# One large buffer more, one split weight tile less, and a changed order, in a hybrid trunk on one core

## The chip, the core and the metric

The kernel runs on one NeuronCore of a Trainium2 chip. The metric is the device time of one execution in microseconds; the median of three runs is given. TensorE (PE) multiplies, VectorE (DVE) and ScalarE (ACT) do the elementwise work, GpSimd (POOL) some small work, SyncE (SP) issues nearly all DMAs.

## What is computed

One layer of a decoder trunk for 512 positions of width 1024, in fp32. A mixer has three branches of width 512 (RG-LRU, gated DeltaNet, S5), each projected, gated and summed. After it come cross-attention into 256 memory positions and a gated MLP with a causal convolution, each with a residual. Cut to the mixer and the memory:

```python
xa, ga, q, k, v, z, beta, alpha, uc, gates = split(h @ w_in)
ya = rg_lru(conv(xa) + b) * gelu(ga)                 # branch 0
o = delta_rule(l2norm(q), l2norm(k), v, g, beta)     # branch 1: per chunk a unit lower triangular solve
yb = rmsnorm(o, b_norm) * silu(z)
yc = gelu(s5(uc)); yc = yc * sigmoid(yc @ w_glu)     # branch 2
x = x + sum(sigmoid(gates) * (branches @ w_branch)) @ w_out
k, v = split(rmsnorm(mem, mem_norm) @ w_kv)          # cross-attention
```

## The kernel before, in words

All weights are 179 tiles of 128x1024 fp32 (512 KB each), in the order of `weight_order()`. SP streams them into a pool `raw` of 3 buffers. ACT rounds a tile into `whi`, DVE takes the rest, raw minus `whi`, into `wlo`; each pool has `WB` buffers. A product is three passes on PE (high by high, high by low, low by high), so a full tile is 24 matmuls of 128x512. `wnext` gives the next tile to PE and splits ahead by `WB - 1` tiles; a split waits until PE is done with the tile that held its buffer.

Large intermediates (8 KB in each partition) live in `NS` slots of one pool, handed out in the order of the program; whoever takes a slot waits for the last reader of what was in it. Small ones of 128x512 come from a pool of 10.

The program text is one run of products (`group`); the S5, RG-LRU, delta and memory parts are Python generators that `pump` advances between the products, by the microseconds that they `yield`. So constants such as `XW`, `HRW` and `MY` say how far along the products the next piece of a side part is put, and Tile's scheduler then sets the order on each engine. Each engine works its own list in that order.

Around the change the order of products is: S5 inputs, keys, queries, values, the RG-LRU inputs XA and GA (tiles 17 to 24), then for each branch `gate` tiles (results `gu`) and `br` tiles (results `psb`). Branch 0 comes first, then branch 2, then the memory's keys (`wk`, `ps_wk`) and values (`wv`, `psv`), the Z tiles and branch 1. Meanwhile on the side:
- `rglru` makes ya: two small products pr and pi, then a chain over ACT (`rg`) and DVE that ends in `yah` and `yal`.
- `s5` writes its kernel `kd` to DRAM and reads it back as a Toeplitz matrix T, forms the states H on DVE, and then multiplies T by U and F by H into `py`.
- `delta` transposes keys, queries and values (`trp`), forms pk and pq per head, solves the triangles on DVE (block substitution in `nBX`, written to DRAM as dX), and later does the rest of the solve on PE (Qp, Zp), the scan over chunks (m, vn, Sp, op), a norm (`oss`), and transposes back (`tro`).
- `mem_prep` waits for the substitution (`sub_done`), loads the memory in one transfer on ACT's DMA queue into a slot, splits it to `mgh` and `mgl`, and makes the norm (`macc`, `rtm`, `rbp`).

```python
mt = self.slot("mem")
nc.scalar.dma_start(out=mt, in_=self.ap["memT"])
```

Of the kernel before, what the change touches and what calls it, by code (L numbers as in the profile page):

```python
# [10 lines left out]
ALU = mybir.AluOpType  # L11
# [3 lines left out]

GA_N = (1, 2, 0)

CH = 1.14
LV = 0.91
XW = 20.0  # L20
VW = 13.0
GW = 20.0
SPD = 30.0
NW = 24.0
MY = 8.0
RW = 9.69
IY = 2.0
VY = 2.41
RY = 2.6
M0 = 2.86  # L30
HY = 2.79
HRW = 7.0
TY = 2.0

NS, NP, WB = 17, 2, 4
WARM = 6
# [3 lines left out]
def weight_order():  # L40
    o = [("uc", t) for t in range(4)]
    for b in (K_, Q_, V_):
        o += [("in", b + t) for t in range(4)]
        if b == Q_:
            o.insert(-3, ("ba",))
    for t in range(4):
        o += [("in", XA + t), ("in", GA + t)]
    for br in (0, 2, 1):
        gt = lambda mp: [("gate", br * 8 + 2 * mp), ("gate", br * 8 + 2 * mp + 1)]
        ahead = GA_N[br]  # L50
        first = [k for mp in range(ahead) for k in gt(mp)]
        if br == 1:
            o += [("wk", m) for m in range(8)]
            o += [("wv", c, kp) for c in range(2) for kp in range(4)]
            o += [("in", Z_ + t) for t in range(4)]
        o += first
        if br == 2:
            o += [("glu", 0), ("glu", 1)]
        for mp in range(4):
            o += (gt(mp) if mp >= ahead else []) + [("br", br, mp)]  # L60
    o += [("out", m) for m in range(8)]
    o += [("wq", m) for m in range(8)]
    o += [("wo", m) for m in range(8)]
# [34 lines left out]
class Kern:  # L98
# [124 lines left out]
    def wnext(self, key, ahead=WB - 1):  # L223
        i = self.wi
        assert ORDER[i] == key, (ORDER[i], key)
        self.wi += 1
        self.w_split(i + 1 + ahead)
        self.w_dma(self.split_i + 2)
        return self.wt.pop(i)
# [156 lines left out]
    def mixer(self, x, xg, rb, pss, par5):  # L386
# [64 lines left out]
        for i in range(4):  # L451
# [6 lines left out]
            self.act(ga, ps, AF.Gelu_apprx_tanh)  # L458
            rgs.append(self.start(self.rglru(i, xf, ga)))
        hbg = cp.tile([128, 24], F32, name="hbg")  # L460
        self.gs(hbg, self.par("b_gate"), 0.5)
        macc = [self.slot("macc0"), self.slot("macc1")]
        mv = lambda m: macc[m // 4][:, (m % 4) * 512:(m % 4 + 1) * 512]
        def gates(br, mp):
            tg = []
            for j in range(2):
                m = 2 * mp + j
                ps = self.group([("gate", br * 8 + m)], h)[0]
                u = self.t512("gu")
                self.act(u, ps, AF.Tanh, scale=0.5, bias=hbg[:, br * 8 + m:br * 8 + m + 1])  # L470
                tg.append(u)
            return tg

        for br in (0, 2, 1):
# [12 lines left out]
            else:  # L487
# [3 lines left out]
                self.mem_values()  # L491
                self.z = self.slot("z")
                for i in range(4):
                    ps = self.group([("in", Z_ + i)], h)[0]
                    self.act(self.z[:, i * 512:(i + 1) * 512], ps, AF.Silu)
                self.z_done = True
                tgs = [gates(br, mp) for mp in range(GA_N[1])]
# [44 lines left out]
    def delta(self):  # L542
# [5 lines left out]

        ktok, vtok = self.slot("ktok"), self.vraw
        ss = sm("ss", 32)  # L550
        for ti, (src, dst) in enumerate(((self.kraw, ktok), (self.qraw, None), (self.vraw, vtok))):
            for h in range(4):
# [4 lines left out]
                if ti < 2:  # L557
                    jk = self.t512("junk")
                    for n in range(4):
                        c = slice(n * 128, (n + 1) * 128)  # L560
                        self.act(jk[:, c], ps[:, c], AF.Square,
                                 accum_out=ss[:, ti * 16 + h * 4 + n:ti * 16 + h * 4 + n + 1])
                if ti != 1:
                    self.act(hv(dst, h), ps)
# [12 lines left out]
        while not self.s5_done:  # L577
            yield

        keT, qeT, kdec = self.kraw, self.qraw, ktok  # L580
        nA, qk = self.slot("nA"), self.slot("qk")
# [3 lines left out]
        yield RW  # L585
        for h in range(4):
            R = E = hv(Rs, h)
            D, DT = self.t512("D"), self.t512("DT")
# [14 lines left out]
            for n in range(4):  # L603
                c = slice(n * 128, (n + 1) * 128)
                self.stt(un(nA, h, n), pk[:, c], nbr[:, h * 4 + n:h * 4 + n + 1], D[:, c], ALU.mult, ALU.mult)
            self.tt(hv(qk, h), pq, DT, ALU.mult)
            self.act(gt[:, h * 4:h * 4 + 4], E[:, 127::128])
            self.tt(hv(qeT, h), hv(qeT, h), E, ALU.mult)
# [36 lines left out]
        for b in range(4):  # L645
            for s in range(2):
                c = 32 * b + 16 * s
                nc.gpsimd.dma_start(out=xv[32 * b:32 * b + 32, :, c:c + 16], in_=dX[s, :, b].rearrange("u i j -> i u j"))
        Z = self.slot("Zi")
        self.gz(Z[:, :1])  # L650
        self.sub_done = True
# [112 lines left out]
        self.tt(o3, o3, rqn, ALU.mult)  # L764
        while not self.z_done:
            yield
        yb = self.kslots("yb", 4)
# [108 lines left out]
    def rglru(self, i, xf, ga):  # L876
        nc = self.nc
        c = slice(i, i + 1)
        wg = self.wg[i % 2]
        yield 4  # L880
        pr, pi = self.psd("pr"), self.psd("pi")
# [179 lines left out]
    def s5(self):  # L1061
# [9 lines left out]
        Q1, Q2 = self.s5Q  # L1071
        self.act(CC[up], CC[up], scale=-1.0)
        yield VW
        Vt = self.slot("Vt0")
        G = self.s5G
        for e in range(4):
# [8 lines left out]
            yield 2.6  # L1085
            if e == 0:
                U = self.slot("U")
                udv = ud.rearrange("(q s) c j n -> s c j q n", s=2)
                for s in range(2):
                    for j in range(4):  # L1090
                        self.sd.dma_start(out=U[64 * s + 16 * j:64 * s + 16 * j + 16, :].rearrange("c (q n) -> c q n", n=128),
                                            in_=udv[s, :, j])
        c4 = self.s5P[:, :64].rearrange("p (o i q) -> p o i q", o=2, i=2)
# [46 lines left out]
        for q in range(16):  # L1140
            self.mm(pk[:, q * 32:(q + 1) * 32], Vt[:, q * 128:(q + 1) * 128], CC[:, q * 32:(q + 1) * 32], True, True)
            if q % 2:
                yield 1.3
        ks = self.t512("ks")
        self.act(ks, pk)
# [8 lines left out]
        for k, e in ((0, 0), (1, 0), (0, 1), (1, 1)):  # L1154
# [6 lines left out]
            for s, rows in enumerate((lo, up)):  # L1161
                self.tt(f5[k][rows, s, q8], ta[rows], tb[rows], ALU.add)
            yield 2.6

        for n, top in ((16, 32), (32, 63)):
# [4 lines left out]
        for e in range(4):  # L1170
            q4 = slice(4 * e, 4 * e + 4)
            ta, tb, tg = (self.t512(n).rearrange("p (o q n) -> p o q n", o=2, q=4) for n in ("ra", "rb5", "rg5"))
            b2 = lambda t: t[:, q4].unsqueeze(1).to_broadcast([128, 2, 4, 64])
# [9 lines left out]
            for o in range(2):  # L1183
                nc.vector.tensor_tensor_scan(out=fl(tg[:, o]), data0=fl(D), data1=fl(wd[:, o, q4]),
                                             initial=0.0, op0=ALU.mult, op1=ALU.add)
            yield TY
            self.tt(ta, b2(C), tg, ALU.mult)
            self.tt(tb, b2(S), tg[:, ::-1], ALU.mult)
            self.tt(wd[:, 0, q4], ta[:, 0], tb[:, 0], ALU.subtract)
            self.tt(wd[:, 1, q4], ta[:, 1], tb[:, 1], ALU.add)  # L1190
            yield TY
        T = self.slot("T")
        self.gz(T, 0.0)
        t5 = T.rearrange("p (q s t d) -> p s q t d", q=16, s=2, t=4)
        for s in range(2):
            for j in range(4):
                r0 = 64 * s + 16 * j
                self.sd.dma_start(out=t5[r0:r0 + 16, s, :, j:], in_=kv[s, :, :, 0:4 - j])
        yield HRW
# [3 lines left out]
        for e in range(4):  # L1203
# [16 lines left out]
            for u in range(4):  # L1220
                c = slice((4 * e + u) * 128, (4 * e + u + 1) * 128)
                d = slice(u * 128, (u + 1) * 128)
                self.mm(ps[:, d], T[:, c], U[:, c], True, False)
                self.mm(ps[:, d], F[0][:, c], H[0][:, d], False, False)
                self.mm(ps[:, d], F[1][:, c], H[1][:, d], False, True)
                yield 0.65
# [242 lines left out]
    def mem_prep(self):  # L1469
        nc = self.nc  # L1470
        while not self.sub_done:
            yield
        yield M0
        mg = self.kslots("mg", 8, 256)
        acc = self.t512("macc")[:, :256]
        mt = self.slot("mem")
        nc.scalar.dma_start(out=mt, in_=self.ap["memT"])
        yield MY
        for k in range(0, 8, 2):
            yield 1.0  # L1480
            for j in range(2):
                xk = mt[:, (k + j) * 256:(k + j + 1) * 256]
                ins = self.split(*mg[k + j], xk, self.par("g_mem")[:, k + j:k + j + 1])
                if k + j == 0:
                    self.tc.keep_in_program_order(ins)
                self.sumsq(acc, k + j, xk, 8, 256)
        self.mg = mg
# [148 lines left out]
```

## Time and profile before

| what | value |
|---|---|
| median of three runs | 1098.15 us (1096.86 to 1098.66) |
| profiled execution, its own time | 1102.97 us |
| its span | 1101.2 us |
| PE busy | 1064.3 us, 97% |
| DVE, ACT, POOL busy | 704.1, 503.3, 149.4 us |
| DMA | 112.30 MB, mean 102 GB/s |

The profiled execution has its own time, beside the span that the engines' records cover. A busy PE can run at either of two clocks; the views give the granted clock of a stretch as a share of full speed (1.00 is 2.4 GHz, and 0.50 would be 1.2 GHz throughout).

### The profile page before, as it was taken

The page shows a single profiled execution, that of the slowest core. Times are in us where ns is not written, and L with a number is a line of the kernel's source. Part 1 is how long each engine was busy: PE and PEld are TensorE (multiplying, and loading weights), DVE is VectorE, ACT ScalarE, POOL GpSimd, SP SyncE. Part 2 cuts the span into 40 slices and gives each one's busy share as a digit, 9 for nine tenths or more (in the row PEclk, how much of TensorE's full clock was granted, in tenths as well). Part 3 has the DMA queues.
Part 4 walks back from the last instruction along what each step waited for, and adds up shares of the span by engine and source line. Part 5 has one row for each costly group of instructions (what it writes and reads, how often), then busy time and mean ns, then how long its engine had stood idle before and what let it go on. Part 6 is the DMA issues. An engine that isn't in the chain of part 4 may idle for free.

```text
span 1101.2 us, 13592 instructions
## 1 busy us (share of the span) xinstructions
PE 1064.3 (97%) x5150; PEld 888.8 (81%) x5150; DVE 704.1 (64%) x1044; ACT 503.3 (46%) x810; POOL 149.4 (14%) x286
## 2 busy tenths in 40 slices
PE   9999998899998799999999999999999999999996
PEld 7778876688886798888888887888888888888886
DVE  6887589937998545356464546487774247777434
ACT  7555676736522435443344435364442124444224
POOL 7898801100001000000000000000000000000003
PEclk9999999899999789999999999999999999999998
DMA  7552222145324313322352112223232322223212
GB/s 251 180 136 78 78 72 77 50 108 199 106 96 142 108 58 115 116 77 96 103 168 93 60 37 96 97 95 97 99 99 100 103 97 97 96 95 96 96 39 77
DMA packets 45633, 112.30 MB, mean 102 GB/s; under 512 B 10608, under 2 KB 18432, under 8 KB 45184
## 3 DMA queue, kind: packets, MB, share of 16 engines
q1 hardware_dynamic: 45168, 110.13, 31.3%
q10 hardware_dynamic: 144, 1.05, 0.3%
q8 instruction: 40, 0.66, 0.2%
q0 software_dynamic: 256, 0.26, 0.1%
q14 instruction: 25, 0.20, 0.1%
HBM read 106.56 MB, written 4.86 MB: 101 GB/s over the span
## 4 chain that ended last, share of the span: by engine, by line
PE 82%; DVE 6%; POOL 5%; DMA 3%; issue 2%; ACT 1%; SPq 0%; DVEq 0%; ACTq 0%; POOLq 0%
PE ps_up L156 24%; PE psdn L156 12%; PE ps_gate L156 9%; PE ps_in L156 7%; PE psb L156 4%; PE ps_wq L156 4%; PE ps_out L156 4%; PE ps_wo L156 4%; POOL s5p L785 3%; PE ps_wk L156 3%; PE psv L156 2%; PE pv L156 2%; DVE wlo L144 1%; PE sc L156 1%; POOL s5p L150 1%
## 5 line engine op out<-in xcount | busy, mean ns | idle before, releaser
L141 ACT ACTIVATE whi<-raw 128x1024 fp32r<-128x1024 f32 (+1 forms) x185 | 189.8, 1030 | 296.5 <-PE psdn L156 79.3
L144 DVE TENSOR_TENSOR wlo<-raw,whi 128x1024 fp32r<-128x1024 f32 (+1 forms) x185 | 219.6, 1192 | 160.4 <-ACT whi L141 153.0
L156 PE MATMUL ps_up<-xgh,wlo 128*128 128x512 f32 x384 | 149.8, 390 | 0.0
L156 PE MATMUL ps_up<-xgh,whi 128*128 128x512 f32 x384 | 149.5, 389 | 0.0
L156 PE MATMUL ps_up<-xgl,whi 128*128 128x512 f32 x384 | 149.4, 389 | 0.0
L144 POOL TENSOR_TENSOR acc<-acc,sq 128x256 f32<-128x256 f32 x11 | 8.3, 752 | 719.8 <-ACT sq L141 719.2
L156 PEld LDWEIGHTS ps_up<-xgh,wlo 128*128 128x128 f32 x384 | 72.1, 188 | 15.2 <-issue 0.2
L156 PEld LDWEIGHTS ps_up<-xgh,whi 128*128 128x128 f32 x384 | 72.1, 188 | 15.0 <-issue 0.2
L156 PEld LDWEIGHTS ps_up<-xgl,whi 128*128 128x128 f32 x384 | 72.1, 188 | 15.0
L156 PE MATMUL psdn<-actl,whi 128*128 128x512 f32 (+1 forms) x216 | 78.9, 365 | 0.0
L156 PE MATMUL psdn<-acth,wlo 128*128 128x512 f32 (+1 forms) x216 | 78.9, 365 | 0.0
L156 PE MATMUL psdn<-acth,whi 128*128 128x512 f32 (+1 forms) x216 | 78.8, 366 | 0.0
L156 PE MATMUL ps_gate<-hh,whi 128*128 128x512 f32 x192 | 76.0, 396 | 1.9 <-ACT gu L141 1.9
L156 PE MATMUL ps_gate<-hh,wlo 128*128 128x512 f32 x192 | 75.6, 394 | 0.0
L156 PE MATMUL ps_gate<-hl,whi 128*128 128x512 f32 x192 | 75.4, 393 | 0.0
L153 DVE SCALAR_TENSOR_TENSOR fu<-pad,par,fu 128x512 f32<-128x512 f32 x96 | 71.5, 748 | 1.8 <-ACT fu L141 0.3
L156 PE MATMUL ps_in<-hh,whi 128*128 128x512 f32 x168 | 68.1, 406 | 0.0
L156 PE MATMUL ps_in<-hh,wlo 128*128 128x512 f32 x168 | 67.2, 400 | 0.0
L156 PE MATMUL ps_in<-hl,whi 128*128 128x512 f32 x168 | 66.9, 398 | 0.0
L144 DVE TENSOR_TENSOR pad<-ps_up,rb 128x512 f32<-128x512 f32 x48 | 32.8, 688 | 43.9 <-PE ps_up L156 42.7
L156 PEld LDWEIGHTS psdn<-actl,whi 128*128 128x128 f32 x216 | 40.7, 189 | 6.6
L156 PEld LDWEIGHTS psdn<-acth,whi 128*128 128x128 f32 x216 | 40.7, 189 | 6.5
(383 smaller groups left out, 2225.9 us busy)
## 6 DMA issues: line engine op xcount, KB each, us to landing
raw<-wts SPq DMA_DIRECT2D x177, 512.0 KB, 3.5
x<-xT SPq DMA_DIRECT2D x16, 256.0 KB, 4.2
out<-x SPq DMA_DIRECT2D x7, 256.0 KB, 2.4
raw<-wts SPq DMA_DIRECT2D x8, 128.0 KB, 4.6
BC<-bc SPq DMA_DIRECT2D x1, 1024.0 KB, 8.1
ud<-uperm SPq DMA_DIRECT2D x4, 256.0 KB, 5.3
U<-ud SPq DMA_DIRECT2D x8, 128.0 KB, 6.0
yd<-T SPq DMA_DIRECT2D x8, 128.0 KB, 3.1
```

The lines of the kernel that those rows point to most:

```text
L141: return self.nc.scalar.activation(out=out, in_=in_, func=func, **k)
L144: return (eng or self.nc.vector).tensor_tensor(out=out, in0=a, in1=b, op=op)
L150: return e.tensor_scalar(out=out, in0=a, scalar1=s1, scalar2=s2, op0=op0, op1=op1)
L153: return self.nc.vector.scalar_tensor_tensor(out=out, in0=a, scalar=s, in1=b, op0=op0, op1=op1)
L156: return self.nc.tensor.matmul(out, lhsT=lhsT, rhs=rhs, start=start, stop=stop)
L785: return self.pin(self.nc.gpsimd.tensor_tensor(out=out, in0=a, in1=b, op=op))
```

## The change

- Buffers: `NS` goes from 17 to 18 slots, `WB` from 4 to 3, and the DMA of weights runs one tile less ahead of the split.
- The four Z tiles are multiplied after the second pair of XA and GA tiles.
- Two pairs of gate tiles, not one, stand ahead of the first `br` tile of branch 0; four of these gate results are kept in a slot `tga`.
- The keys' slot `ktok` is taken later; the keys are transposed a second time (`trk`, 4 transposes a head) in the loop that makes pk and pq. The four ACT copies move along.
- T is taken and cleared right behind the S5 kernel's product, and its eight loads are issued from ACT's queue, not SP's. The products of `py` start with F and H. U is loaded earlier.
- The memory is loaded in four transfers into four small tiles; its split goes into two slots (`mg0`, `mg1`) that hold high and low parts side by side.
- Yield constants change (XW 20 to 30, VW 13 to 10, NW 24 to 20, IY 2.0 to 1.6, HRW 7 to 4, TY 2.0 to 2.4, two yields in place of waits), and one S5 temporary goes.

```diff
-GA_N = (1, 2, 0)
+GA_N = (2, 2, 0)
-NS, NP, WB = 17, 2, 4
+NS, NP, WB = 18, 2, 3
...
         o += [("in", XA + t), ("in", GA + t)]
+        if t == 1:
+            o += [("in", Z_ + t) for t in range(4)]
...
             o += [("wv", c, kp) for c in range(2) for kp in range(4)]
-            o += [("in", Z_ + t) for t in range(4)]
         o += first
...
         self.w_split(i + 1 + ahead)
-        self.w_dma(self.split_i + 2)
+        self.w_dma(self.split_i + 1)
         return self.wt.pop(i)
...
             rgs.append(self.start(self.rglru(i, xf, ga)))
+            if i == 1:
+                self.z = self.slot("z")
+                for j in range(4):
+                    ps = self.group([("in", Z_ + j)], h)[0]
+                    self.act(self.z[:, j * 512:(j + 1) * 512], ps, AF.Silu)
+                self.z_done = True
         hbg = cp.tile([128, 24], F32, name="hbg")
...
+        tga = self.slot("tga")
...
-                u = self.t512("gu")
+                u = tga[:, m * 512:(m + 1) * 512] if br == 0 and m < 4 else self.t512("gu")
...
-                if ti != 1:
+                if ti == 2:
                     self.act(hv(dst, h), ps)
...
+        ktok = self.slot("ktok")
...
+            pt = self.psd("trk")
+            for n in range(4):
+                self.tr(pt[:, n * 128:(n + 1) * 128], un(self.kraw, h, n))
...
             self.tt(hv(qk, h), pq, DT, ALU.mult)
+            self.act(hv(ktok, h), pt)
...
+        T = self.slot("T")
+        self.gz(T, 0.0)
...
+        t5 = T.rearrange("p (q s t d) -> p s q t d", q=16, s=2, t=4)
+        for s in range(2):
+            for j in range(4):
+                r0 = 64 * s + 16 * j
+                nc.scalar.dma_start(out=t5[r0:r0 + 16, s, :, j:], in_=kv[s, :, :, 0:4 - j])
...
-                self.sd.dma_start(out=t5[r0:r0 + 16, s, :, j:], in_=kv[s, :, :, 0:4 - j])
...
-                self.mm(ps[:, d], T[:, c], U[:, c], True, False)
-                self.mm(ps[:, d], F[0][:, c], H[0][:, d], False, False)
-                self.mm(ps[:, d], F[1][:, c], H[1][:, d], False, True)
+                self.mm(ps[:, d], F[0][:, c], H[0][:, d], True, False)
+                self.mm(ps[:, d], F[1][:, c], H[1][:, d], False, False)
+                self.mm(ps[:, d], T[:, c], U[:, c], False, True)
...
-        yield M0
-        mg = self.kslots("mg", 8, 256)
+        sl = [self.slot(f"mg{i}", F32R) for i in range(2)]
+        mg = [tuple(sl[k // 4][:, (2 * (k % 4) + z) * 256:(2 * (k % 4) + z + 1) * 256] for z in range(2)) for k in range(8)]
         acc = self.t512("macc")[:, :256]
-        mt = self.slot("mem")
-        nc.scalar.dma_start(out=mt, in_=self.ap["memT"])
+        ms = [self.t512("mem") for _ in range(4)]
+        for i, m in enumerate(ms):
+            nc.scalar.dma_start(out=m, in_=self.ap["memT"][:, i * 512:(i + 1) * 512])
         yield MY
-        for k in range(0, 8, 2):
-            yield 1.0
-            for j in range(2):
-                xk = mt[:, (k + j) * 256:(k + j + 1) * 256]
-                ins = self.split(*mg[k + j], xk, self.par("g_mem")[:, k + j:k + j + 1])
-                if k + j == 0:
-                    self.tc.keep_in_program_order(ins)
-                self.sumsq(acc, k + j, xk, 8, 256)
+        for k in range(8):
+            xk = ms[k // 2][:, k % 2 * 256:(k % 2 + 1) * 256]
+            ins = self.split(*mg[k], xk, self.par("g_mem")[:, k:k + 1])
+            if k == 0:
+                self.tc.keep_in_program_order(ins)
+            self.sumsq(acc, k, xk, 8, 256)
+            if k % 2:
+                yield 1.0
+        self.gz(self.Zi[:, :1])
         self.mg = mg
         rt, _ = self.rstd([acc], n=256, bc=False)
         yield RY

```

How that moves instructions shows in the lists of the engines. On PE, at the first branch product of the program before (`whi_1741` is a gate tile, `whi_1802` the first `br` tile, weight 27):

```order
L156 MATMUL ps_gate<-hl_436,whi_1741 128x512
L156 MATMUL ps_gate<-hh_434,wlo_1742 128x512
L156 MATMUL psb<-yah_1274,whi_1802 128x512
L156 MATMUL psb<-yal_1275,whi_1802 128x512
L156 MATMUL psb<-yah_1274,wlo_1803 128x512
L156 MATMUL pr<-xfga,wg_695 128x512
```

After the change the gate tiles (`whi_2022` is the third, weight 31) lead to `py`, and the first `br` tile (`whi_2166`, weight 33) stands behind the last `py`:

```order
L157 MATMUL ps_gate<-hh_426,whi_2022 128x512
L157 MATMUL ps_gate<-hl_428,whi_2022 128x512
L157 MATMUL py_2040<-H_1997,F_1350 128x128
L157 MATMUL py_2040<-H_1998,F_1351 128x128
L157 MATMUL py_2040<-U,T 128x128
...
L157 MATMUL py_2256<-U,T 128x128
L157 MATMUL psb<-yah_1257,whi_2166 128x512
L157 MATMUL psb<-yal_1258,whi_2166 128x512
```

Before, `psb` came after two gate tiles and `py` later, between other tiles; after, the four Z tiles and three gate tiles come first, then `py` among the fourth, then `psb`.

On ACT, at the memory's load before (`whi52` and `whi53` are weights of the memory's keys, `gu` gate results; what a row waits for stands in brackets, DMAHW1 in the first DMA row is the landing of dX):

```order
L141 ACTIVATE whi52_3113<-raw52_3035 128x1024 [waits DMAHW5_49,DVE_49,PE_49]
L141 ACTIVATE gu_3110<-ps_gate_3073,hbg_1862 128x512 [waits PE_49]
L141 ACTIVATE whi53_3158<-raw53_3078 128x1024 [waits DMAHW6_49,DVE_49,PE_49]
L141 ACTIVATE gu_3156<-ps_gate_3112,hbg_1862 128x512 [waits PE_49]
L1477 DMA mem_3174<-memT 128x2048 [waits DMAHW1_49,DVE_49]
L141 ACTIVATE whi54_3248<-raw54_3117 128x1024 [waits DMAHW7_49,PE_49,Activation_49]
L141 ACTIVATE mgh0_3171<-mem_3174,par_84 128x256 [waits DMAHW2_49]
```

and after (`whi51` is a `br` tile, `whi54` the last one of branch 2; DMAHW5 in the `mg1` row is the landing of dX):

```order
L142 ACTIVATE gu_3067<-ps_gate_3030,hbg_2016 128x512 [waits PE_49]
L1484 DMA mem_3115<-memT 128x512
L1484 DMA mem_3116<-memT 128x512
L1484 DMA mem_3117<-memT 128x512
L1484 DMA mem_3118<-memT 128x512 [waits DVE_49]
L142 ACTIVATE whi51_3133<-raw51_3073 128x1024 [waits DMAHW4_49,DVE_49,PE_49]
L142 ACTIVATE mg0_3112<-mem_3115,par_84 128x256 [waits DMAHW7_49]
...
L142 ACTIVATE gu_3241<-ps_gate_3165,hbg_2016 128x512 [waits DVE_49,PE_49]
L142 ACTIVATE mg1_3113<-mem_3117,par_84 128x256 [waits DMAHW5_49,DVE_49]
L142 ACTIVATE mg1_3113<-mem_3117,par_84 128x256
L142 ACTIVATE mg1_3113<-mem_3118,par_84 128x256 x2
L142 ACTIVATE whi54_3292<-raw54_3247 128x1024 [waits DMAHW3_49,PE_49]
```

The transfers and half of the split moved four gate and branch tiles ahead; `mg1`, which takes the slot of `nBX`, still stands behind dX, and `whi54` behind `mg1`.

On PE, at the memory's norm before (`whi_3248` is weight 54, a tile of the memory's keys):

```order
L156 MATMUL ps_wk<-mgh_3171,whi_3248 128x256
L156 MATMUL ssp<-cst,macc 128x1 x2
L156 MATMUL ps_wk<-mgl_3172,whi_3248 128x256
L156 MATMUL ps_wk<-mgh_3171,wlo_3249 128x256
L156 MATMUL rbp<-diag,cst 128x256
L156 MATMUL Qp<-Zi,nA 96x64 x16
```

and after (`whi_3166` and `whi_3243` are gate tiles 52 and 53, `whi_3292` is the `br` tile 54, `whi_3325` the first tile of the memory's keys):

```order
L157 MATMUL ps_gate<-hh_426,whi_3166 128x512
L157 MATMUL ssp<-cst,macc 128x1 x2
L157 MATMUL ps_gate<-hl_428,whi_3166 128x512
...
L157 MATMUL ps_gate<-hh_426,whi_3243 128x512
L157 MATMUL rbp<-diag,cst 128x256
L157 MATMUL ps_gate<-hl_428,whi_3243 128x512
...
L157 MATMUL psb<-ych_2740,wlo_3293 128x512
L157 MATMUL ps_wk<-mg_3112,whi_3325 128x256 x2
```

The two small products of the norm, `ssp` and `rbp`, moved from the middle of the keys' tiles to the gate tiles ahead of them.

## Rows read from the trace of the kernel before

**Rows 1.** The page, busy time (share of the span) and instructions of the engines.
```profile
PE 1064.3 (97%) x5150; PEld 888.8 (81%) x5150; DVE 704.1 (64%) x1044; ACT 503.3 (46%) x810; POOL 149.4 (14%) x286
```
**Rows 2.** PE's waits, whole kernel: who waited for whom, us, times, longest.
```profile
PE ps_wk L156 <- ACT mgh L141: 8.8, 1, 8.8
PE rbp L156 <- DVE rtm L1493: 3.2, 1, 3.2
```
**Rows 3.** Windows, us: busy (instructions) of PE, PEld, DVE, ACT, POOL; clock; DMA share; GB/s.
```profile
180.00:200.00 20.00, 11.73 (x35) 7.19 (x34) 19.88 (x35) 13.56 (x16) 6.77 (x5) 0.86 0.23 80
200.00:220.00 20.00, 18.12 (x82) 14.86 (x81) 19.77 (x37) 13.83 (x25) 2.28 (x6) 0.88 0.17 43
...
340.00:360.00 20.00, 13.07 (x58) 10.50 (x56) 14.20 (x18) 4.33 (x5) 4.73 (x7) 0.96 0.54 167
360.00:380.00 20.00, 14.87 (x104) 14.47 (x105) 12.55 (x25) 10.86 (x22) 0.77 (x2) 0.84 0.23 66
380.00:400.00 20.00, 20.00 (x145) 19.33 (x145) 7.58 (x14) 5.35 (x11) 0.00 (x0) 0.60 0.19 60
...
720.00:740.00 20.00, 20.00 (x90) 16.57 (x89) 17.95 (x25) 11.76 (x16) 0.00 (x0) 1.00 0.32 105
```
**Rows 4.** Timeline of PE, first branch products: start, us, instruction, count, [idle before <-releaser].
```profile
185.19 0.39 PE L156 MATMUL psb<-yal,whi 128*128 128x512 f32 x1
185.41 0.39 PE L156 MATMUL psb<-yah,wlo 128*128 128x512 f32 x1
190.86 1.90 PE L156 MATMUL pr<-xfga,wg 128*128 128x512 f32 x2 [5.06 <-ACT rg L141]
```
**Rows 5.** Timeline (start us, us, engine), the entry to the memory's keys.
```profile
297.20 0.09 DVE L626 MEMSET nBX<- 128x32 f32 x1
...
349.30 0.33 SPq L639 DMA_DIRECT2D dX<-nBX  x1
...
352.68 0.39 PE L156 MATMUL psb<-ych,wlo 128*128 128x512 f32 x1
353.46 0.37 ACTq L1477 DMA_DIRECT2D mem<-memT  x1
...
361.88 1.22 PE L156 MATMUL ps_wk<-mgh,whi 128*128 128x256 f32 x4 [8.82 <-ACT mgh L141]
```
**Rows 6.** DMA issues: transfer, queue, count, KB each, median us to landing.
```profile
x<-xT SPq DMA_DIRECT2D x16, 256.0 KB, 4.2
mem<-memT ACTq DMA_DIRECT2D x1, 1024.0 KB, 7.8
```
**Rows 7.** The page's groups for the two halves of the weight split: count, busy, mean ns, idle before.
```profile
L141 ACT ACTIVATE whi<-raw 128x1024 fp32r<-128x1024 f32 (+1 forms) x185 | 189.8, 1030 | 296.5 <-PE psdn L156 79.3
L144 DVE TENSOR_TENSOR wlo<-raw,whi 128x1024 fp32r<-128x1024 f32 (+1 forms) x185 | 219.6, 1192 | 160.4 <-ACT whi L141 153.0
```
**Rows 8.** Timeline of PE, the first gate tile and the first S5 output.
```profile
174.08 0.39 PE L156 MATMUL ps_gate<-hh,whi 128*128 128x512 f32 x1
...
216.90 0.38 PE L156 MATMUL py<-U,T 128*128 128x128 f32 x2
```
**Rows 9.** Tiles H and T: engine, count, ns min/median/max, first and last start.
```profile
L144 DVE TENSOR_TENSOR H<-ha,Ve x8: 413/414/423, 211.1 to 227.7; 128x252 f32<-128x252 f32 x8
L1198 SPq DMA_DIRECT2D T<-kd x8: 601/608/612, 208.7 to 213.3; - x8
```
**Rows 10.** The pq products of the delta heads by form: count, busy, mean ns.
```profile
L156 PE MATMUL pq<-qraw,kraw 128*128 128x128 f32 x32 | 6.3, 278 | 0.1
```
**Rows 11.** Timeline of PE, ACT and DVE, the last delta outputs to their norm.
```profile
463.92 0.39 PE L156 MATMUL op<-vnew,qk 128*128 128x128 f32 x2
...
468.07 0.31 ACT L141 ACTIVATE oss<-oss,eps 128x16 f32<-128x16 f32 x1
...
468.92 2.49 DVE L144 TENSOR_TENSOR qraw<-qraw,oss 128x512 f32<-128x512 f32 x4
471.33 1.22 DVE L144 TENSOR_TENSOR wlo<-raw,whi 128x1024 fp32r<-128x1024 f32 x1
```

More of the change, by code (lines that the diff above doesn't have):

```diff
@@ L14 @@
 EPS = 1e-6
-GA_N = (1, 2, 0)
+GA_N = (2, 2, 0)
 CH = 1.14
 LV = 0.91
-XW = 20.0
-VW = 13.0
+XW = 30.0
+VW = 10.0
 GW = 20.0
 SPD = 30.0
-NW = 24.0
+NW = 20.0
 MY = 8.0
 RW = 9.69
-IY = 2.0
+IY = 1.6
 VY = 2.41
@@ L31 @@
 HY = 2.79
-HRW = 7.0
-TY = 2.0
-NS, NP, WB = 17, 2, 4
+HRW = 4.0
+TY = 2.4
+NS, NP, WB = 18, 2, 3
 WARM = 6
@@ L491, in mixer @@
                 self.mem_values()
[L492 to L496, printed above, removed]
                 tgs = [gates(br, mp) for mp in range(GA_N[1])]
@@ L547, in delta @@
         u4 = lambda t: t.rearrange("p (n c) -> p n c", n=4)
-        ktok, vtok = self.slot("ktok"), self.vraw
+        vtok = self.vraw
         ss = sm("ss", 32)
-        for ti, (src, dst) in enumerate(((self.kraw, ktok), (self.qraw, None), (self.vraw, vtok))):
+        for ti, (src, dst) in enumerate(((self.kraw, None), (self.qraw, None), (self.vraw, vtok))):
             for h in range(4):
@@ L648, in delta @@
                 nc.gpsimd.dma_start(out=xv[32 * b:32 * b + 32, :, c:c + 16], in_=dX[s, :, b].rearrange("u i j -> i u j"))
-        Z = self.slot("Zi")
-        self.gz(Z[:, :1])
+        Z = self.Zi = self.slot("Zi")
         self.sub_done = True
@@ L764, in delta @@
         self.tt(o3, o3, rqn, ALU.mult)
-        while not self.z_done:
-            yield
+        yield 6
         yb = self.kslots("yb", 4)
@@ L879, in rglru @@
         wg = self.wg[i % 2]
-        yield 4
+        yield 6
         pr, pi = self.psd("pr"), self.psd("pi")
@@ L1072, in s5 @@
         self.act(CC[up], CC[up], scale=-1.0)
+        yield 6
+        U = self.slot("U")
+        udv = ud.rearrange("(q s) c j n -> s c j q n", s=2)
+        for s in range(2):
+            for j in range(4):
+                self.sd.dma_start(out=U[64 * s + 16 * j:64 * s + 16 * j + 16, :].rearrange("c (q n) -> c q n", n=128),
+                                  in_=udv[s, :, j])
         yield VW
@@ L1085, in s5 @@
             yield 2.6
[L1086 to L1092, printed above, removed]
         c4 = self.s5P[:, :64].rearrange("p (o i q) -> p o i q", o=2, i=2)
@@ L1163, in s5 @@
             yield 2.6
+        t5 = T.rearrange("p (q s t d) -> p s q t d", q=16, s=2, t=4)
+        for s in range(2):
+            for j in range(4):
+                r0 = 64 * s + 16 * j
+                nc.scalar.dma_start(out=t5[r0:r0 + 16, s, :, j:], in_=kv[s, :, :, 0:4 - j])
         for n, top in ((16, 32), (32, 63)):
@@ L1171, in s5 @@
             q4 = slice(4 * e, 4 * e + 4)
-            ta, tb, tg = (self.t512(n).rearrange("p (o q n) -> p o q n", o=2, q=4) for n in ("ra", "rb5", "rg5"))
+            ta, tb = (self.t512(n).rearrange("p (o q n) -> p o q n", o=2, q=4) for n in ("ra", "rb5"))
             b2 = lambda t: t[:, q4].unsqueeze(1).to_broadcast([128, 2, 4, 64])
@@ L1183, in s5 @@
             for o in range(2):
-                nc.vector.tensor_tensor_scan(out=fl(tg[:, o]), data0=fl(D), data1=fl(wd[:, o, q4]),
+                nc.vector.tensor_tensor_scan(out=fl(ta[:, o]), data0=fl(D), data1=fl(wd[:, o, q4]),
                                              initial=0.0, op0=ALU.mult, op1=ALU.add)
             yield TY
-            self.tt(ta, b2(C), tg, ALU.mult)
-            self.tt(tb, b2(S), tg[:, ::-1], ALU.mult)
+            self.tt(tb, b2(S), ta[:, ::-1], ALU.mult)
+            self.tt(ta, b2(C), ta, ALU.mult)
             self.tt(wd[:, 0, q4], ta[:, 0], tb[:, 0], ALU.subtract)
@@ L1191, in s5 @@
             yield TY
[L1192 to L1197, printed above, removed]
-                self.sd.dma_start(out=t5[r0:r0 + 16, s, :, j:], in_=kv[s, :, :, 0:4 - j])
         yield HRW
```

## The prediction

> **What bounds the kernel now.** I read the busy shares first, then PE's waits, then windows of 20 us, then the timeline where a window was not full. PE is busy for 97% of the span and no other engine for more than 64% [rows 1], so an edit pays only where PE stands still or runs at the lower clock. The table of waits names few such places: 8.8 us at the first product of the memory's keys and 3.2 at the memory's norm [rows 2]. The windows show what surrounds them. Two stretches stand out, and an MLP window (720 to 740) shows the full rate to compare with: PE 20.00 of 20 us, 90 matmuls, clock 1.00 [rows 3].
>
> Stretch A is 180 to 220 us, at branch 0. PE is idle for 8.27 and 1.88 us, and the granted clock is 0.86 and 0.88; at full clock those windows would have held 0.14 x 20 + 0.12 x 20 = 5.2 us more of work. Lost: at most 10.2 + 5.2 = 15.4 us. DVE is at 19.88 and 19.77 of 20 there, so ya comes late; the branch product starts, stops, and PE waits 5.06 us [rows 4].
>
> Stretch B is 340 to 400 us. Idle: 6.93, 5.13 and 0. Clock 0.96, 0.84, 0.60: 0.8 + 3.2 + 8.0 = 12.0 us. Lost: at most 24.1 us [rows 3]. The timeline gives the chain: the substitution ends, dX leaves at 349.30; the memory's transfer, which waits until it has landed, leaves at 353.46 and takes 7.8 us; the split `mgh` follows, and PE, which had run dry behind 352.68, starts at 361.88 [rows 5, 6].
>
> So 39.5 us is a ceiling on what can be won at these two places (idle time at low clock is counted in it twice, so it is rather 38.6, which I get by spacing of matmuls, 0.23 us at full clock [rows 4]). I use 39.5 and let the doubt stand in the range.
>
> **The change, part by part.**
>
> *Stretch A.* The gates of branch 0 start at 174.1 and py at 216.9 before [rows 8]. Four Z tiles of 24 x 0.227 = 5.4 us now stand ahead of the gates, 21.8 us in all; less a pr/pi pair of 1.9 us that moves behind, the gates start near 194. Another 62 gate matmuls and one pair, 16 us, lead to py: about 210. The first H was ready from 211.1 [rows 9]; DVE's list ahead of it is 1.4 us shorter when each of its rows is priced by the same row's duration before, so H comes near 210. T's loads no longer wait for the scan (208.7 to 213.3 before) [rows 9]: they are ready long before. The branch product stands behind py, at about 229, when ya, needed at 185 before, has had 44 us more. I take the stall as gone, and 2 us for short waits of py on H. Bounds: none, and 10 us if DVE is as late as before (rival 3).
>
> T's eight loads cost ACT 8 x 0.6 = 4.9 us of issue [rows 9]; they stand where PE has Z tiles to work on and splits two tiles ahead. None of it reaches PE; without that cover it would be those 4.9 us.
>
> *The second transposing of the keys* is 16 PE instructions. The nearest row is the pq product of the same kind and form, 32 in 6.3 us of overlapping records, spaced 0.11 us [rows 10]: 16 x 0.11 = 1.8 us, all on PE. Its ACT copies take the place of the old ones.
>
> *Stretch B.* PE reached the keys' product at 352.9; now it has four Z tiles more behind it (21.8), 1.8 of transposes, 2 of small waits, less 15.4: about 363. DVE's substitution ran from 297.20 to 349.30, 52 us [rows 5]. By the count of PE's rows ahead of the last pk its inputs come some 5 to 7 us earlier, so it ends near 342 to 344, and dX, 4.2 us later as before, lands near 347. The memory no longer takes a slot that dX must free: it leaves in four parts four tiles earlier, and half its split with it. Only `mg1` waits for dX; that is some 15 us ahead of need, and `whi54`, queued behind `mg1`'s four instructions on ACT, some 2 us, has about 6 us to spare. The norm's two products sit among gate tiles, so the 3.2 us wait goes too. With no hole PE stays at clock 1.00 and the 12 us come back. Four transfers: one of 256 KB lands in 4.2 us, the whole in 7.8 [rows 6], so the first part is there no later than the whole was, and the last has 15 us. Cost nothing; without the cover 4.2 us.
>
> The Trainium skill, DMA: Bandwidth & Descriptors, section Rules for kernel authors, speaks against this edit: many small transfers should be made one large one, because each pays a fixed cost. By its figure of about 2 us for that, three more would be an estimate of 6 us and the sum would still be the same, since the cover is larger. The trace agrees that a quarter costs more than a quarter of the time.
>
> *Where the stall goes next.* With the Z tiles gone from behind the memory's values, the delta scan and the transposing back lose their cover. From the last op product (463.92) to the norm's root takes 4.4 us, to the scaled outputs 4.4 to 7.5, and the next low half ends at 472.55, 8.6 us later [rows 11]. PE's list now holds 18 value matmuls (4.1), 2 more (0.45) and 16 transposes (1.8), 6.35 us, before it needs that low half: 2.6 us of wait including the ACT split behind the root. Where m meets vn with nothing between, one eviction and subtraction, about 1.2 us. Bounds for this corner: 0, and 8.6 if nothing covers it.
>
> *Three split tiles.* A tile's low half is ready whi + wlo = 1.03 + 1.19 us after its buffer comes free [rows 7]. With four buffers that is 3 x 5.44 - 2.2 = 14.1 us ahead of need, with three 8.7. DVE waited for `whi` in 153 of 160 us of its idle time ahead of `wlo` [rows 7]: it is there when the tile comes. So nothing in the MLP. In the attention's output product, where three tiles are held open at once and the next three need their buffers one after the other, I charge a high and a low split not covered, less the little that is lost today: 1.8 us (bounds 0 and 2 x 2.2).
>
> Sum: 39.5 - 1.8 - 2 - 2.6 - 1.2 - 1.8 = 30.1 us. Against the profiled execution: 1102.97 - 30.1 = 1072.9 (span near 1071). That execution is 4.8 us over the median of the runs, so the forecast for the median is 1098.15 - 30.1 = **1068**.
>
> **Rivals.** A result within 0.2% (2.2 us) of before can't be told from no change.
>
> 1. *Nearly all of it comes.* The new waits are covered: 39.5 - 1.8 = 37.7, so 1060.5. For it: ACT and DVE are 46% and 64% busy [rows 1]. Against: the corner behind the values has rows that add up to more than PE's work.
>
> 2. *The new waits stay and pull the clock down.* If the substitution ends as late as before, dX lands at 353.4, `mg1` ends at 355.5, `whi54` and `wlo54` at 357.7 [rows 5, 7], at about the time its tile is due (357.5); any lateness in the keys' tiles, whose matmuls are half as wide and so leave half the time for a split, is paid in full. A hole in the keys or values costs like the one before: half of stretch B's clock loss, 6 us, beside 5 us of idle. That leaves 19 us: 1079. For it: 0.60 was granted behind two waits of 8.82 and 3.24 us [rows 3, 5]; on ACT's list `whi54` stands behind `mg1` and can't pass it.
>
> 3. *Stretch A only moves.* DVE stays full, H comes at 217 as py did, and PE waits at py as it did at pr: 5 us, and 5 of clock. Gain 20 us, 1078. Against: DVE's list is shorter there and ya is not asked for.
>
> 4. *Slower.* Three split tiles starve PE in the MLP. Its 72 tiles would have to lose 37.7 / 72 = 0.52 us each to eat the whole. This starts once DVE work ahead of a low half passes 8.7 us. DVE is busy 17.95 of 20 us in an MLP window [rows 3], that is 9.8 us in the 10.9 us of two tiles, 7.4 of them not splits: if all of that stood ahead of one split, 7.4 + 1.2 = 8.6, just at the edge. One us a tile past it gives 1098 - 30 + 72 = 1140; half of that, 1104. Against: the low halves waited for ACT, not for DVE [rows 7].
>
> That the change does not do what it says: the orders on PE and ACT have already moved; only the times can fail.
>
> **How the numbers follow.** Forecast (1063 to 1074) 0.5; rival 1 (1058 to 1063) 0.13; rivals 2 and 3 together (1074 to 1088) 0.25; both at once or a partial starvation (1088 to 1096) 0.03; no change 0.03; slower 0.06. The range 1060 to 1085 leaves out what lies above 1085 (some 0.13) and part of rival 1 (0.06). Faster 0.91, same 0.03, slower 0.06.
>
> **What would show it.** Right: windows 180 to 240 with PE at 20 us; no wait of ps_wk on ACT and clock 1.00 from 340 to 400; `ps_gate` of branch 1 some 28 us earlier; waits of 1 to 3 us at `tro`, vn or psv, and at ps_wo. Wrong: a wait of py on H over 4 us; ps_wk or the last psb waiting for `mgh` or `whi`; PE waiting for DVE's `wlo` in the MLP, window after window.

## The result, and the profile after

The changed kernel takes 1072.76 us (median of 4 runs, 1072.69 to 1072.97); the kernel before took 1098.41 beside it (1096.86 to 1098.74). The ratio is 0.977, 95% interval 0.9753 to 0.9787: 25.7 us less. The forecast was 1068, with a range from 1060 to 1085.

The profiled execution of after took 1072.72 us with a span of 1070.9. Against the profiled execution of before (1102.97, span 1101.2) that is 30.3 us, where the sum had said 30.1. So in the traces the sum came out, in part by luck, as the first experiment shows; the 4.8 us by which the median missed its forecast lie in carrying the sum over from the profiled execution to the median.

The windows of the changed kernel answer to [rows 3]. Columns: window, us; busy us (instructions) of PE, its weight load, DVE, ACT, POOL; granted clock; DMA share; GB/s.

```profile
180.00:200.00 20.00, 18.75 (x79) 14.45 (x78) 20.00 (x34) 11.29 (x14) 0.42 (x1) 1.00 0.28 97
200.00:220.00 20.00, 19.42 (x106) 15.94 (x105) 19.25 (x35) 14.32 (x31) 1.14 (x8) 1.00 0.24 80
...
340.00:360.00 20.00, 18.79 (x86) 15.34 (x85) 14.77 (x28) 11.31 (x17) 5.38 (x8) 1.00 0.55 150
360.00:380.00 20.00, 20.00 (x205) 19.55 (x204) 13.37 (x20) 7.01 (x10) 0.10 (x1) 1.00 0.35 113
380.00:400.00 20.00, 20.00 (x182) 19.67 (x182) 11.99 (x24) 10.40 (x22) 0.00 (x0) 1.00 0.31 99
...
420.00:440.00 20.00, 16.95 (x91) 13.47 (x90) 11.99 (x20) 11.22 (x23) 0.00 (x0) 1.00 0.28 90
...
720.00:740.00 20.00, 20.00 (x90) 16.57 (x89) 15.84 (x20) 9.17 (x11) 0.00 (x0) 1.00 0.26 84
```

Idle time in 180 to 220 is 1.83 us (10.15 before), in 340 to 400 it is 1.21 (12.06 before), and the clock is 1.00 in all of them. DVE is as full as it was in 180 to 220: it does no less there, but PE no longer asks it for ya. The new gap is 3.05 us of idle time in 420 to 440, and the MLP window is full.

PE's waits in the changed kernel: who waited for whom, us, times, longest. They answer to [rows 2].

```profile
PE ps_gate L157 <- DVE vs L154: 1.7, 1, 1.7
PE warm L157 <- DVE pad L347: 1.5, 1, 1.5
PE ps_uc L157 <- ACT xgh L142: 1.4, 1, 1.4
PE pr L157 <- DVE xfga L154: 1.3, 1, 1.3
PE ssp L157 <- DVE macc L145: 1.2, 1, 1.2
PE rbp L157 <- DVE diag L145: 1.2, 1, 1.2
PE psv L157 <- ACT whi L142: 0.9, 1, 0.9
PE pbt L441 <- ACT bt L142: 0.7, 1, 0.7
PE py L157 <- DVE H L145: 0.6, 1, 0.6
```

No wait is longer than 1.7 us; the longest was 8.8. The `rbp` row is at the end of the kernel, as it was before.

The timeline of the changed kernel (start, us, engine) at the memory's keys answers to [rows 5]:

```profile
320.57 0.87 ACTq L1484 DMA_DIRECT2D mem<-memT  x2
321.46 0.94 ACTq L1484 DMA_DIRECT2D mem<-memT  x2
...
343.65 0.33 SPq L647 DMA_DIRECT2D dX<-nBX  x1
346.34 1.71 ACT L142 ACTIVATE mg<-mem,par 128x256 fp32r<-128x256 f32 x4 [3.62 <-DVE macc L145]
347.96 1.04 ACT L142 ACTIVATE whi<-raw 128x1024 fp32r<-128x1024 f32 x1
...
360.58 0.39 PE L157 MATMUL psb<-ych,wlo 128*128 128x512 f32 x1
360.81 0.40 PE L157 MATMUL ps_wk<-mg,whi 128*128 128x256 f32 x2
```

The memory leaves 23 us ahead of dX, not 4 us behind it. The second half of its split follows dX at 346.34, and PE passes from the branch tile to the keys at 360.81 without a gap, 14 us later.

The delta's end, on PE, with the idle time ahead of each instruction and its releaser:

```profile
431.18 0.73 PE L157 MATMUL psv<-whi,mg 128*128 128x512 f32 x2 [0.94 <-ACT whi L142]
434.40 0.50 PE L157 MATMUL psv<-wlo,mg 128*128 128x512 f32 x1 [0.41 <-DVE wlo L145]
438.65 0.50 PE L157 MATMUL ps_gate<-hh,whi 128*128 128x512 f32 x1 [1.69 <-DVE vs L154]
```

Those three are the price of having moved the Z tiles away from here: they were cover, work that PE can do while it would otherwise wait. The run below that puts them back, with one pair of gate tiles ahead, has none of the three waits.

### The profile page after: what moved, and what is told of

Read it like the earlier page. It is cut to its first block, busy times and chain, and to the rows that moved or that the text cites. A ratio compares the mean times of both kernels' runs of the same rounds, so it can differ in the third digit from the quotient of the medians.

```text
span 1070.9 us, 13581 instructions
## 1 busy us (share of the span) xinstructions
PE 1051.4 (98%) x5166; PEld 877.8 (82%) x5166; DVE 705.2 (66%) x1044; ACT 502.7 (47%) x812; POOL 143.0 (13%) x286
## 4 chain that ended last, share of the span: by engine, by line
PE 80%; DVE 9%; POOL 5%; ACT 3%; issue 2%; DMA 0%; SPq 0%; ACTq 0%; DVEq 0%; POOLq 0%
PE ps_up L157 24%; PE psdn L157 12%; PE ps_gate L157 10%; PE psb L157 5%; PE ps_wq L157 4%; PE ps_out L157 4%; PE ps_wo L157 4%; PE ps_in L157 4%; POOL s5p L791 3%; PE ps_wk L157 2%; DVE wlo L145 2%; PE pv L157 2%; PE psv L157 1%; PE sc L157 1%; PE psg L157 1%
## 5 line engine op out<-in xcount | busy, mean ns | idle before, releaser
L145 DVE TENSOR_TENSOR wlo<-raw,whi 128x1024 fp32r<-128x1024 f32 (+1 forms) x185 | 219.6, 1190 | 136.9 <-ACT whi L142 131.5
L157 PEld LDWEIGHTS psdn<-acth,wlo 128*128 128x128 f32 x216 | 40.7, 189 | 6.6
```

The lines of the kernel that those rows point to most:

```text
L145: return (eng or self.nc.vector).tensor_tensor(out=out, in0=a, in1=b, op=op)
L157: return self.nc.tensor.matmul(out, lhsT=lhsT, rhs=rhs, start=start, stop=stop)
```

## The experiments

The medians of before beside these runs were 1096.2 to 1096.5 us, with single runs from 1091.67 to 1104.0; ratios are against them. The changed kernel was not timed again beside these runs: where a run is set against it, its 1072.76 us from the first timing is meant, and before's median was some 2 us higher there (1098.41). Against the later medians of before the change is worth 23.4 to 23.8 us, not 25.7.

**The kernel before once more, unchanged.**

> The kernel before, unchanged, profiled once more. The profiled execution of before took 1102.97 us where the median of its runs was 1098.4; that of the changed kernel took just its median. Theory: the idle time of the two stretches (22 us in the windows 180 to 220 and 340 to 400) is the same in every execution, and what differs is how long the clock stays low behind it; so where this execution is shorter than 1102, its clock in 180 to 220 and 340 to 400 is higher by the same microseconds (0.14 + 0.12 + 0.04 + 0.16 + 0.40 of 20 us each before), and the idle time within 1 us of before. Rival: the profile costs this kernel 4.6 us each time; then this execution takes 1102.5 to 1103.5 us with the clocks of before.

It took 1099.19 us, span 1097.4. Two rows of that execution, PE at the keys and at the norm:

```profile
358.11 1.22 PE L156 MATMUL ps_wk<-mgh,whi 128*128 128x256 f32 x4 [5.83 <-ACT mgh L141]
375.01 1.16 PE L156 MATMUL rbp<-diag,cst 128*128 128x256 f32 x2 [3.24 <-DVE rtm L1493]
```

and the memory's transfer in its DMA view (queue, count, KB, us to landing):

```profile
mem<-memT ACTq DMA_DIRECT2D x1, 1024.0 KB, 4.8
```

Its windows in the two stretches, in the columns of [rows 3]:

```profile
180.00:200.00 20.00, 11.87 (x34) 7.14 (x33) 19.77 (x36) 12.91 (x15) 6.77 (x5) 0.77 0.21 76
200.00:220.00 20.00, 16.85 (x88) 13.67 (x87) 19.86 (x37) 14.72 (x28) 2.39 (x7) 0.98 0.17 43
...
340.00:360.00 20.00, 14.17 (x64) 11.72 (x63) 15.12 (x20) 6.78 (x12) 5.49 (x9) 0.86 0.56 182
360.00:380.00 20.00, 16.76 (x121) 16.35 (x121) 13.82 (x27) 9.78 (x19) 0.00 (x0) 0.84 0.30 98
380.00:400.00 20.00, 20.00 (x166) 19.11 (x166) 6.85 (x14) 5.28 (x11) 0.00 (x0) 0.70 0.10 38
```

Neither theory was right. The idle time was not the same: the transfer took 4.8 us here and 7.8 in [rows 6], and PE waited 5.8 us where it had waited 8.8. By the windows the clock gave back nothing in sum (A 5.0 us against 5.2, B 12.0 against 12.0), though it lay otherwise. Idle time and clock together, the two stretches lost 37.4 us here and 39.4 in the execution that I had read. That is 2 of the 3.8 us between the two. More lies in a window that I had not looked at, 60 to 80, first as in the execution read for the prediction, then as here:

```profile
60.00:80.00 20.00, 18.06 (x79) 13.09 (x78) 19.07 (x28) 10.16 (x18) 19.01 (x23) 0.91 0.59 120
60.00:80.00 20.00, 19.29 (x92) 14.20 (x91) 18.50 (x26) 10.72 (x18) 19.01 (x23) 1.00 0.61 134
```

The changed kernel has 19.25 us of PE and clock 1.00 there. So by the same count some 3 us of the 30.3 between the profiled executions come from a place for which the sum has no term.

Two other versions below keep the memory's one transfer. With three split tiles:

```profile
PE ps_wk L156 <- ACT mgh L141: 7.7, 1, 7.7
mem<-memT ACTq DMA_DIRECT2D x1, 1024.0 KB, 6.7
```

and with the norm's products drawn apart:

```profile
PE ps_wk L156 <- ACT mgh L141: 6.9, 1, 6.9
mem<-memT ACTq DMA_DIRECT2D x1, 1024.0 KB, 5.9
```

In all four executions PE's wait at the keys is the time of the transfer plus 1.0 us. The runs of the kernel before spread over 12 us, and the execution that I had read stands near the slow end. The transfer's time is one part of that spread; that it is the whole is not shown.

**The memory part alone, on the kernel before.** `mem_prep` as after, all else as before:

```diff
...
-        mt = self.slot("mem")
-        nc.scalar.dma_start(out=mt, in_=self.ap["memT"])
+        ms = [self.t512("mem") for _ in range(4)]
+        for i, m in enumerate(ms):
+            nc.scalar.dma_start(out=m, in_=self.ap["memT"][:, i * 512:(i + 1) * 512])
...
```

> The kernel before with the changed memory part alone (four transfers into small tiles, two slots of which the second waits for dX). Theory: the wait of 8.8 us at the keys goes, the wait at the norm shrinks, and with them the low clock behind them; the Z tiles still cover the delta's end. 12 us idle plus 7 to 12 us of clock: 1077 to 1084 us. Rival: the end of the substitution (dX) binds, not the memory's transfer, and the reordered tiles are what matters: then the gain is under 6 us, 1092 to 1098.

1089.77 us, ratio 0.994 (0.9912 to 0.9968): 6.7 us less, under the theory's 12 to 19 and just over the rival's bound. Three of PE's rows there, with its waits:

```profile
355.14 0.39 PE L156 MATMUL ps_wk<-mg,whi 128*128 128x256 f32 x1 [0.37 <-DVE mg L153]
365.50 0.61 PE L156 MATMUL ssp<-cst,macc 128*128 128x1 f32 x4 [0.56 <-DVE macc L144]
369.58 0.94 PE L156 MATMUL rbp<-diag,cst 128*128 128x256 f32 x2 [3.48 <-DVE rtm L1494]
```

The wait at the keys is gone (0.37 us for 5.8 to 8.8), so the transfer, which could leave only behind dX, held them, and not dX itself. The norm's wait of 3.5 us stays, for `ssp` and `rbp` stand side by side on PE, and with it a clock of 0.83 in 360 to 380. Both parts of stretch B need their own cure.

**The changed kernel with stretch A undone.** Z tiles behind the memory's values, one pair of gate tiles ahead:

```diff
-GA_N = (2, 2, 0)
+GA_N = (1, 2, 0)
...
-        if t == 1:
-            o += [("in", Z_ + t) for t in range(4)]
...
             o += [("wv", c, kp) for c in range(2) for kp in range(4)]
+            o += [("in", Z_ + t) for t in range(4)]
...
```

> The changed kernel with the Z tiles behind the memory's values again and one pair of gate tiles ahead in branch 0 (stretch A undone, the rest kept). Theory: PE comes to the branch product too early again, idles about 10 us and runs some 5 us at low clock, and the 3 us at the delta's end are covered again: plus 8 to 14 us, 1081 to 1087. Rival: DVE's shorter S5 list and the earlier loads of T removed stretch A by themselves: 1070 to 1075.

1081.04 us, 0.9852 (0.9812 to 0.9892): 8.3 us more than the changed kernel, at the low end of the theory. Idle in 180 to 220 is 9.08 us again, at clock 0.91 and 0.85, but there is no gap at the delta's end:

```profile
180.00:200.00 20.00, 16.21 (x60) 12.00 (x60) 16.99 (x29) 17.02 (x23) 2.27 (x4) 0.91 0.18 63
200.00:220.00 20.00, 14.71 (x66) 12.42 (x64) 19.30 (x35) 9.30 (x21) 1.17 (x8) 0.85 0.16 53
```

**The same with two pairs of gate tiles ahead**, so Z alone put back.

> The changed kernel with the Z tiles behind the memory's values as before, but two pairs of gate tiles ahead in branch 0 as changed. Theory: each tile ahead of the branch product gives it 5.4 us of time, whichever tile it is; with two gate tiles more than in the run with one pair, PE waits less: 1076 to 1080. Rival: Z ahead is what matters (its 21.8 us): no better than with one pair, 1080 to 1083.

1101.39 us, 1.004 (1.0024 to 1.0056), worse than either theory. In 180 to 220 it loses as much as with one pair (8.10 us idle). The rest is lost later: dX leaves at 366.3 us, where it left at 352.8 with one pair, between 350 and 371 PE waits 6.4 us on the memory's split and the norm's sums and 1.4 us on DVE at the keys, and the transposes at the delta's end wait 6.3 us. So in this order gate tiles are not cover of the same worth as Z tiles; why the delta part ends so much later behind them stays open.

**The changed kernel with the memory part of before.** The diff of the memory part, reversed.

> The changed kernel with the memory part of before (one transfer that waits for a slot, split behind it). Theory as predicted: the memory's own transfer made the wait: it can leave at about 348 when dX has landed, its first split is ready at 356, the last near 363, against a need at 360.8 and the norm in the middle of the keys: 2 to 6 us of waits and some clock, 1074 to 1082. Rival: the Z tiles, moved ahead, are all that stretch B needed: 1071 to 1074. Second rival: all of stretch B returns: above 1085.

1080.85 us, 0.9853 (0.982 to 0.9886): 8.1 more, at the top of the theory, but at another place than it said. ACT and PE:

```profile
343.82 0.39 ACTq L1484 DMA_DIRECT2D mem<-memT  x1
...
353.25 0.42 ACT L142 ACTIVATE macc<-mem 128x256 f32<-128x256 f32 x1 [7.85 <-DMA mem<-memT]
...
354.49 0.67 ACT L142 ACTIVATE gu<-ps_gate,hbg 128x512 f32<-128x512 f32 x1
```

```profile
355.21 0.79 PE L157 MATMUL ps_gate<-hh,whi 128*128 128x512 f32 x1 [7.14 <-ACT gu L142]
```

ACT stands for 7.85 us at the landing of the memory; the gate result behind it in ACT's list comes only then. PE's next gate product, which needs a bank of PSUM (where products are gathered) that ACT has read, waits 7.14 us for it.

**The same, with what needs the memory put later on ACT.**

```diff
-MY = 8.0
+MY = 22.0
```

> The changed kernel with the memory in one transfer as before, but its squares and split put 14 us of products later, so that on ACT the first instruction that needs the memory stands behind the gate results that PE needs. Theory: in the run with one transfer PE lost 7.1 us because ACT works in order and stood at the landing of the memory with a gate result queued behind; with those gate results ahead of it, that wait goes: 1073 to 1077. Rival: the one large transfer is simply late, and the wait moves to the norm or the keys' product: 1079 to 1083.

1080.82 us, 0.9842 (0.982 to 0.9864): the rival. The gate wait is gone, and PE waits at the norm's sums instead, with a clock of 0.74 in 360 to 380:

```profile
365.04 0.98 PE L157 MATMUL ssp<-cst,macc 128*128 128x1 f32 x4 [5.38 <-DVE macc L145]
```

Where ACT waits decides where PE stands still; that it stands still is common to both runs, and in both the one transfer leaves only when dX has freed its slot, 2.1 us behind it (343.82 and 344.4 us). Four transfers into a slot, or one into a buffer that is free early, were not run, so what the number of transfers does by itself is not shown.

**Three split tiles, on the kernel before.** One constant: `WB` 4 to 3.

> The kernel before with three split weight tiles in place of four, nothing else. Theory: the low half of a tile is ready 8.7 us ahead in place of 14.1 and DVE is there when it comes, so the MLP loses nothing and the whole is within 3 us of before (a few us at the memory's values and at the attention's output). Rival 4 of the prediction: the MLP starves, 0.5 us or more a tile: above 1130.

1090.58 us, 0.9948 (0.9925 to 0.9971). The MLP does not starve. But the kernel gets 5.6 us faster, outside the 3 us that I allowed: with three tiles the scheduler puts the 24 matmuls of one keys' tile between `ssp` and `rbp`, and the 3.2 us wait is gone from the trace.

**That norm alone, on the kernel before.** One constant, `RY` 2.6 to 5.2, puts the 16 Qp products between the two, where only two products of the keys stood.

> The kernel before with one constant changed, so that 18 products more (the first solve's Qp) stand between the norm's two small products. It tests why three split tiles alone gave 5.6 us: their order has 24 matmuls there and no wait. Theory: the wait of 3.2 us at rbp and the low clock behind it go: minus 3 to 6 us, 1090 to 1094 beside a before of 1096. Rival: the gain came from the split buffers themselves: within 1.5 us of before.

1092.41 us, 0.9968 (0.9949 to 0.9987), 4.1 us less: the wait at `rbp` falls from 3.2 to 1.1 us, and clock comes back:

```profile
380.00:400.00 20.00, 19.68 (x201) 18.98 (x202) 11.65 (x21) 8.72 (x15) 0.00 (x0) 1.00 0.25 84
```

A change of order alone gives 4.1 us where three split tiles gave 5.6, and the two intervals overlap. So the order that the split tiles brought can be most of their gain; that it is all of it is not shown.

**The changed kernel with the keys transposed once.** `ktok` is taken and filled early as before; the 16 later transposes go.

```diff
...
-        vtok = self.vraw
+        ktok, vtok = self.slot("ktok"), self.vraw
...
-            pt = self.psd("trk")
-            for n in range(4):
-                self.tr(pt[:, n * 128:(n + 1) * 128], un(self.kraw, h, n))
...
```

> The changed kernel with the keys transposed once: the copy is kept in its slot from the first transposing on, and the 16 later transposes go. Theory: they cost PE 1.8 us and the eighteen slots have room: 1070.5 to 1071.5. Rival: a slot is short meanwhile and some later tile waits for it: 1074 or more.

1101.47 us, 1.0046 (1.0025 to 1.0067): 28.7 us more, not 1.8 less; the rival had said 1074 or more. One wait on PE:

```profile
194.13 0.79 PE L157 MATMUL ps_in<-hh,whi 128*128 128x512 f32 x1 [23.83 <-ACT z L142]
```

**The changed kernel with 17 slots and four split tiles.**

```diff
-NS, NP, WB = 18, 2, 3
+NS, NP, WB = 17, 2, 4
```

> The changed kernel with the buffers of before, 17 large ones and four split tiles. Theory: what counts is the order, but the order needs the slot: somewhere between branch 0 and the delta's end a slot comes free later than its taker is due, and PE waits 2 to 15 us: 1074 to 1087. Rival: the eighteenth slot is not needed, and the deeper split even gives back the waits of the values and the output product: 1068 to 1072.

1101.28 us, 1.0033 (1.001 to 1.0056), worse than either theory, and the same wait:

```profile
195.19 0.79 PE L157 MATMUL ps_in<-hh,whi 128*128 128x512 f32 x1 [24.27 <-ACT z L142]
```

In both, the slot for Z comes free only when DVE's S5 work is done with it, near 193.5 and 194.5; PE, whose next products need the PSUM banks that ACT's `z` reads, waits for it, and 28 us are lost in all with the clock at 0.83 to 0.86 and 0.54 to 0.57. The early Z tiles need both slots: the one that the third split tile gave, and the one that the later `ktok` leaves free meanwhile.

**Two further steps.** Two gate tiles of branch 1 between the halves of the memory's values (`wv`), as cover for the delta's end:

```diff
...
-            o += [("wv", c, kp) for c in range(2) for kp in range(4)]
+            o += [("wv", 0, kp) for kp in range(4)] + [("gate", 8), ("gate", 9)]
+            o += [("wv", 1, kp) for kp in range(4)]
...
```

> The changed kernel with the first two gate tiles of branch 1 between the two halves of the memory's values. Theory: the 3 us of waits at the delta's end are lack of cover; 24 gate matmuls more between the last op product and the transposes cover the norm's chain: minus 2.5 to 3.5 us, 1069.3 to 1070.3. Rival: the chain only ends later behind them, or the gate's own split is late with three buffers: 1072 to 1074.

1070.38 us (1069.59 to 1072.28), 0.9761 (0.9715 to 0.9808). The three waits of the delta's end are gone; one of 1.0 us at a gate tile behind the keys takes their place. The median is 2.4 us below that of the changed kernel, but the interval of this ratio holds the changed kernel's 0.977, so a gain in time is not shown. Then, on top, the memory's norm put 3 us later (a yield ahead of `rstd`):

> The changed kernel with the two gate tiles between the halves of the memory's values, and the memory's norm put 3 us of products later, against the 1.6 us that PE waits there for the sum of squares. Theory: that wait goes, minus 1 to 2 us against the version without it: 1068 to 1069.5. Rival: the norm's end is then late for the keys, or the wait is only moved: 1070 to 1072.

1070.13 us (1070.04 to 1070.21), 0.9746 (0.9726 to 0.9767); the wait at the norm went from 1.6 to 1.1 us, and the time is the rival's. It has the lowest median here, but its interval too overlaps that of the changed kernel (0.9753 to 0.9787), and from each other the two can't be told apart.

## Why the prediction was right, and where it was off

- **Stretch A.** H came at 207.8 us (210 forecast), py at 208.5 (210), the branch product at 229.6 (229). The short waits came to 1.83 us where 2 were forecast, but only 0.58 of it was the wait of py on H that the text named; 1.25 was at pr. Undoing the stretch cost 8.3 us, less than the 15.4 of the window sum. In that run 180 to 220 loses 9.08 us of idle time and 4.8 of clock, 12.1 more than the changed kernel, and 1.0 more at the norm's sum, but it is spared 3.5 us at the delta's end: 9.6 by this count, in which idle time at low clock stands twice.
- **T's loads on ACT** left at 140.3 to 145.3 us and cost PE nothing visible, as said: PE has no wait from 110 to 180. This was not tried apart, nor were the yield constants or the order within py.
- **Stretch B.** dX left at 343.65 (342 to 344 forecast), the keys started at 360.8 (363), and the clock stayed at 1.00. That the four transfers cost nothing holds: they land in 3.2 to 5.9 us, some 33 us ahead of the keys' product. The Trainium skill's rule (DMA: Bandwidth & Descriptors, Rules for kernel authors) to coalesce many small transfers would have one here. With one the kernel was 8 us slower, but that run changed the buffer too: the small tiles start without a slot, the large one waits for dX. So it is the early start that is shown to pay; what four transfers cost against one, all else equal, no run here shows.
- **The delta's end.** 2.6 + 1.2 us forecast; 0.94 + 0.41 + 1.69 and 0.44 at vn measured, 3.5. The sum fits better than its parts: the 1.69 at the gate tile, which waits for DVE's `vs`, was not named, and vn took 0.44 where 1.2 was said. The waits are gone in the run with Z put back and one pair of gate tiles, and in the run with gate tiles between the values, so lack of cover is their cause.
- **Three split tiles.** No starvation: DVE waited for `whi` in 131.5 of 136.9 us of its idle time ahead of `wlo`, as in [rows 7]. The output product of the attention cost 1.0 us more, from its first matmul to its last 55.4 us for 54.4; 1.8 was forecast.
- **Not foreseen:** 1.21 us at the norm's sum of squares.
- **Mis-sized: the step from the profiled execution to the median.** The text took 30.1 us off both. Off the execution that was read, that gives 1072.9, and 1072.76 came; off the median it gives 1068. The execution that was read held losses that others do not have: a wait of 8.8 us on a transfer of 7.8, where another held 5.8 on 4.8, and some 3 us in 60 to 80. The ceiling of 39.5 us was that of a slow execution, and of the median it should have been less by what that execution lay above it, 4.6 us, which gives 25.5. That is not a second proof, since it is the 1072.9 once more. And since the 30.1 had no term for 60 to 80, that 30.3 came in the traces is luck in part.
- **The parts were costed apart, and are not.** The second transposing was a cost of 1.8 us in the sum, the split tile one of 1.8. Each holds up a gain of 28 us, for without either slot the Z tiles wait 24 us. The sum was right because all parts were there.

## What to carry to other kernels

A buffer that is freed by doing small work twice (16 transposes) can be worth many times that work, if the order of the large work hangs on it: price such edits together, by the wait that comes when one is left out. Where the engine that bounds the kernel stands still in one profiled execution, ask first how that wait varies over executions; here one on a transfer ran from 5.8 to 8.8 us. And cover is moved, not made: ask what was standing behind the tiles that go.

## What I had not expected of the hardware

The same 1 MB transfer on the same queue took 7.8 us in one execution of the kernel before and 4.8 in another, and PE waited 3.0 us less. The runs of that kernel spread from 1091.67 to 1104.0 us, while four runs of the changed kernel lay within 0.3. That the transfer makes the whole spread is not shown: with the memory in four transfers and Z put back behind two pairs of gate tiles, the runs spread from 1099.9 to 1104.92. The wait of 3.2 us at the norm, behind that of 8.8, was followed by a clock of 0.60 over 20 us in [rows 3]; with products put between, and a wait of 6.9 us at the keys still there, the same stretch was granted 1.00, and 360 to 380 still 0.88.
